# Two-layer decoder trunk in one kernel: 20 sums over partitions as products with rounded ones, and no product of zeros ahead of a chunk

## The chip, the cores and the metric

The kernel runs on one core of one Trainium2 chip. The metric is device time in microseconds (us) of one execution; the time of a kernel is the median of its runs. The engines are PE (TensorE, matrix products; PEld is its weight load), DVE (VectorE), ACT (ScalarE), POOL (GpSimd) and SP (SyncE, which here issues DMAs).

## What is computed

A trunk of two layers over 16 meta tokens and 512 tokens, with model width 1024 and hidden width 2816. Each layer is a gated FFN, a token mixer and another gated FFN; layer 0 mixes by chunked gated linear attention with four heads, layer 1 by sliding-window attention on one shared key/value set. Everything is float32. What matters here is that every sub-layer is wrapped in two norms over the model width, and that the four heads of the linear attention have a norm of their own:

```
def rmsnorm(x, g):
    y = x * rsqrt(mean(x * x, axis=-1) + EPS);  return y * g
def swiglu(x, w_in, w_out):
    gate, up = split(x @ w_in, 2);  return (silu(gate) * up) @ w_out
h = h + 0.5 * rmsnorm(swiglu(rmsnorm(h, g[0]), ...), g[1])      # first FFN
h = h + rmsnorm(mixer(rmsnorm(h, g[2])), g[3])
h = h + 0.5 * rmsnorm(swiglu(rmsnorm(h, g[4]), ...), g[5])      # second FFN
# inside the linear attention, per head:  o = rmsnorm(o, g_head) * silu(r)
```

## The kernel before

Features lie on the 128 partitions and tokens along the free axis, so the residual `H` is eight tiles of 128 features by 528 tokens. Tokens are worked in two groups: 272 and 256 in layer 0 (`L0`), 256 and 256 in layer 1 (`L1`). Precision of float32 in the matrix products comes from splitting: each operand `x` is kept as a part in the rounded format (`F32R`, printed fp32r) and a remainder, `x - rounded(x)`, also in that format. ACT makes the first with a Copy, DVE the second with a subtraction. A product is then three matmuls (`mm3s`): high by high, low by high, high by low.

The norm factors are not applied ahead of a product but behind it. `Operand.build` splits `H` times the gain; `Operand.sumsq` squares each of the eight tiles on ACT and adds them up on POOL (L394) into one tile `acc` of 128 partitions; `Operand.factors` waits `FACT` = 5 us of the planned clock and calls `roots`. That one sums `acc` over the partitions with a product by a matrix of `ones` in plain float32 (tile `st_...` on the PSUM side), and behind it takes the reciprocal root on ACT (L375, L376) and refines it on DVE (L377 to L379). The result `R` scales what comes out of the projections. There are six such operands with factors of their own (l0f0, l0m, l0f1, kv, l1m, l1f1) of two groups each: 12 sums. The four heads of the linear attention make 8 more (`st_go`, in `core`, behind `square_into`). The norms on the way back into the residual (`Residual.run`, `st_post`) use `roots` too.

The FFNs work their first four hidden tiles plainly (`x_first`, `x_units`) and the other 18 in three chunks with a scheme of seven products in place of eight (class `Strassen`). It keeps five PSUM banks per chunk: two each of `a` and `c`, which alternate between hidden tiles, and one `d`. For each hidden tile, `head` forms product 11 in `a` and copies it on ACT into `d` (L871); `body` adds product 12 onto `d` and takes Silu of it into `g1` (L880). Before the first tile of a chunk, the constructor multiplies zeros by zeros into `d`, once for each of the 12 chunks, so that what ACT writes there can be added onto by the products behind it.

The order of work is written out by hand: a planned clock (`flow`) advances with each matmul issued, and generators that `yield` a delay put ACT, DVE and POOL work between the matmuls at planned times. Each engine's own list is then ordered by what a planner holds to be ready, so that work issued later can stand ahead. Each engine is then given its list, with waits on semaphores in it.

Of the kernel before, what the change touches and what calls it, by code (L numbers as in the profile page):

```python
# [9 lines left out]
F32 = mybir.dt.float32  # L10
F32R = mybir.dt.float32r
I32 = mybir.dt.int32
AF = mybir.ActivationFunctionType
ALU = mybir.AluOpType
AX = mybir.AxisListType

P = 128
D = 1024
# [9 lines left out]
L0 = [(0, 272), (272, 256)]  # L28
# [11 lines left out]
FACT = 5.0  # L40
# [87 lines left out]
def trunk_kernel(ctx: ExitStack, tc, a, out):  # L128
    nc = tc.nc
    pe, act, dve, pool, sp = nc.tensor, nc.scalar, nc.vector, nc.gpsimd, nc.sync  # L130
    flow = Flow()

    cp = ctx.enter_context(tc.tile_pool(name="cp", bufs=1))
    rp = ctx.enter_context(tc.tile_pool(name="rp", bufs=RAWS))
    hp = ctx.enter_context(tc.tile_pool(name="hp", bufs=SLOTS))
    sm = ctx.enter_context(tc.tile_pool(name="sm", bufs=3))
# [5 lines left out]
    ident = cp.tile([P, P], F32, name="ident")  # L142
    ones = cp.tile([P, P], F32, name="ones")
    eps = cp.tile([P, 1], F32, name="eps")
    zeros = cp.tile([P, P], F32R, name="zeros")

    def ps(name):
        return pp.tile([P, 512], F32, tag="ps", name=name)

    def pair_tile(name, dt=F32R):  # L150
        return hp.tile([P, 2, TOK], dt, tag="pair", name=name)
# [5 lines left out]
    def flat(t):  # L157
        return t.rearrange("p a t -> p (a t)")
# [5 lines left out]
    def mm(o, lhs, rhs, start=True, stop=True, onto=False):  # L164
        inst = pe.matmul(o, lhs, rhs, start=start, stop=stop, skip_group_check=onto)  # L165
        n = 1
        for d in rhs.shape[1:]:
            n *= d
        flow.clock += n / 2400 if rhs.dtype == F32R else max(n / 600, 0.12)
        return inst  # L170
# [161 lines left out]
    def next_pair():  # L332
        used[0] += 1
        prefetch()
        flow.until(lambda: len(loaded) >= used[0])
        return loaded[used[0] - 1]
# [27 lines left out]
        mm3s([(o, w)], j, x, g, start, stop)  # L364


    def roots(sums, n, c, name, dst=None, dim=D):
        s = ps(f"st_{name}")
        for i, t in enumerate(sums):
            mm(s[:, :n], ones, t[:, :n], i == 0, i == len(sums) - 1)  # L370
        yield SUMMED
        if dst is None:
            dst = (sums[1] if sums[1:] else acc_tile(f"root_{name}"))[:, :n]
        q, y = sums[0][:, :n], dst
        act.activation(y, s[:, :n], AF.Abs_reciprocal_sqrt, scale=1.0 / dim, bias=eps)  # L375
        act.activation(q, y, AF.Square, scale=dim ** -0.5)  # L376
        dve.scalar_tensor_tensor(q, s[:, :n], dim * 1e-6, q, op0=ALU.add, op1=ALU.mult)  # L377
        dve.tensor_scalar(q, q, -0.5 * c, 1.5 * c, op0=ALU.mult, op1=ALU.add)
        dve.tensor_tensor(y, q, y, op=ALU.mult)  # L379
        return y, s  # L380


    def acc_tile(name):
        return sm.tile([P, 272], F32, tag="acc", name=f"acc_{name}", bufs=6)

    def square_into(sums, src, i, count, name, apart=False):
        n = src.shape[-1]
        if i == 0 or apart and i == count - 1:
            sums.append(acc_tile(name))
            act.activation(sums[-1][:, :n], src, AF.Square)  # L390
            return
        t = sm.tile([P, 272], F32, tag="sq", name=f"sq_{name}", bufs=2)
        act.activation(t[:, :n], src, AF.Square)  # L393
        pool.tensor_tensor(sums[0][:, :n], sums[0][:, :n], t[:, :n], op=ALU.add)  # L394
# [6 lines left out]
    class Operand:  # L401


        def __init__(self, name, gv, groups, rt=None):
            self.name, self.gv, self.groups, self.tiles = name, gv, groups, [None] * KD
            self.ready = set()
            self.rt = rt
            self.rjob = [None] * len(groups)
            self.built = [Job(None) for _ in groups]
            self.accs = [[] for _ in groups]  # L410
# [17 lines left out]
        def factors(self, gi):  # L428
            if self.rt is None:
                self.rt = sm.tile([P, TOK], F32, tag="R", name=f"R_{self.name}", bufs=2)  # L430
            o, n = self.groups[gi]
            yield FACT
            yield from roots(self.accs[gi], n, 1.0, f"{self.name}_{o}", self.rt[:, o : o + n])

        def need(self, gi, k):
            flow.until(lambda: (gi, k) in self.ready)
# [2 lines left out]
    class Residual:  # L439
# [4 lines left out]
        def run(self, gi, g, sums):  # L444
            o, n = g
            nxt = self.nxt
            yield 1.8
            r, s = yield from roots(sums, n, self.c, f"post_{self.name}{gi}")
            if nxt is None:
                yield from self.store(gi, g, r)  # L450
                return
            for k in range(KD):
                h, y = H[:, k, o : o + n], Y[:, k, o : o + n]
                c = k % 2 * 256
                t = s[:, c : c + n] if n <= 256 else ps(f"t_{self.name}{gi}{k}")[:, :n]
                dve.scalar_tensor_tensor(t, y, self.gain(k), r, op0=ALU.mult, op1=ALU.mult)
                dve.tensor_tensor(h, t, h, op=ALU.add)  # L457
                nxt.build(gi, k)
                nxt.sumsq(gi, k)
                yield 1.0  # L460
            nxt.rjob[gi] = flow.spawn(nxt.factors(gi))
            nxt.built[gi].finish(flow)
# [374 lines left out]
    class Strassen:  # L837
        def __init__(self, z, halves):
            self.z, (self.o, self.n) = z, halves[0]
            self.a, self.c = ([ps(f"{nm}{used[0]}_{i}")[:, : self.n] for i in range(2)] for nm in "ac")  # L840
            self.d = ps(f"d{used[0]}")[:, : self.n]
            q = self.n // 4
            zz = zeros[:, :q].unsqueeze(1).to_broadcast([P, 4, q])
            mm(self.d.rearrange("p (a c) -> p a c", c=q), zeros, zz)
            self.tiles = []

        def product(self, bank, t, left, right, first):
# [13 lines left out]
        def head(self, hid):  # L861
            t = Job(None)
            t.pair, t.hid, i = next_pair(), hid, len(self.tiles) % 2
            self.tiles.append(t)
            t.a, t.c, t.name = self.a[i], self.c[i], used[0]
            scratch = flat(pair_tile(f"c{t.name}", F32))
            n = self.n
            t.u2, t.g1, t.v = (scratch[:, i * n : (i + 1) * n] for i in range(3))
            t.h = scratch[:, n : 3 * n]
            self.product(t.a, t, "11", "11", True)  # L870
            act.activation(self.d, t.a, AF.Copy)  # L871
            return t

        def body(self, t):
            self.product(t.c, t, "s1", "t1", True)
            act.activation(t.v, t.c, AF.Copy)
            self.product(t.a, t, "s2", "t2", False)
            act.activation(t.u2, t.a, AF.Copy)  # L878
            self.product(self.d, t, "12", "21", False)
            act.activation(t.g1, self.d, AF.Silu)  # L880
            self.product(t.a, t, "s3", "t3", False)
            dve.tensor_tensor(t.v, t.a, t.v, op=ALU.add)

# [28 lines left out]
    def gla(x, finish):  # L912
        set_ahead(10)
        with tc.tile_pool(name="gp", bufs=1) as gp:
# [61 lines left out]
            def core(h, before):  # L976
# [10 lines left out]
                for i in range(2):  # L987
                    p = ps(f"pv{h}_{i}")
# [32 lines left out]
                p = ps(f"pk{h}")  # L1021
# [13 lines left out]
                p = ps(f"pa{h}")  # L1035
# [14 lines left out]
                s = flat(pair_tile(f"st{h}", F32))[:, :1024].rearrange("p (b v) -> p b v", v=256)  # L1050
                p = ps(f"ps{h}_0")
# [11 lines left out]
                for i in range(2):  # L1063
                    vs = slice(i * P, (i + 1) * P)
                    p = ps(f"po{h}_{i}")
                    for b in range(4):
                        o = p[:, b * P : (b + 1) * P]
# [7 lines left out]
                accs = []  # L1075
                for gi, (o, n) in enumerate(L0):
                    accs.append([])
                    for i in range(2):
                        square_into(accs[gi], Y[:, 2 * h + i, o : o + n], i, 2, f"go{h}_{gi}")
                yield 2.0  # L1080
                def scale(gi, o, n):
                    r, _ = yield from roots(accs[gi], n, 0.5, f"go{h}_{gi}", dim=256)
                    dve.tensor_tensor(
                        yy[:, :, o : o + n], yy[:, :, o : o + n],
                        r.unsqueeze(1).to_broadcast([P, 2, n]), op=ALU.mult,
                    )
# [50 lines left out]
            for h in range(HEADS):  # L1137
                cores.append(flow.spawn(core(h, [gate] + late + cores[h - 1 : h])))
                if h + 1 < HEADS:
                    kk = [("k", h + 1), ("q", h + 1), ("v", 2 * h + 2), ("v", 2 * h + 3)]  # L1140
                    late = x_units(x, 4, L0, lambda i, g, p, kk=kk: evac(*kk[i], g, p))
# [206 lines left out]


    dve.memset(ones, 1.0)  # L1350
    act.activation(zeros, ones, AF.Copy, scale=0.0)
    act.dma_start(vec, a["vec"])
    x = Operand("l0f0", lambda k: gain(0, 0, k), L0)

# [12 lines left out]
    def second():  # L1367
        for k in range(KD):
            x.build(1, k)
            yield 0.4  # L1370
        x.rjob[1] = flow.spawn(factors(1))
# [14 lines left out]
    for c in (0, 512):  # L1386
        for k in range(c // 128, c // 128 + 4):
            x.build(0, k)
            if k % 4 < 2:
                split_part(k % 4, raws[k % 4][c // 512], 512)  # L1390
    x.rjob[0] = flow.spawn(factors(0), 2.0)
    dma_end[0] = 1.0
    load_unit()
# [131 lines left out]
```

## Time and profile before

| | before |
|---|---|
| median of 3 runs | 1869.87 us (1869.71 to 1871.39) |
| the profiled execution | 1868.85 us |
| its span, first to last instruction | 1867.0 us |
| PE busy | 1848.1 us (99%) |
| DVE, ACT, POOL busy | 1349.2, 1002.0, 315.2 us (72%, 54%, 17%) |
| mean granted TensorE clock | 0.999 |

The span is what the profile sees; 1.85 us of the profiled execution lie around it. Busy times of engines overlap. L165 is the line of the helper that issues every matmul, so products are told apart by their tiles. A sum in plain float32 appears as two records of one matmul each.

### The profile page before, as it was taken

How to read it: one execution, taken by the hardware profiler on the slowest of the kernel's cores; microseconds unless marked ns; L12 is line 12 of the kernel's file. 1: busy time of each engine (PE TensorE's matmuls, PEld its weight loads, DVE VectorE, ACT ScalarE, POOL GpSimd, SP SyncE). 2: the span in 40 equal slices, each digit the busy share in tenths (PEclk: the TensorE clock that was granted, in tenths of full speed). 3: DMA queues.
4: the chain of work that ended last, by engine and by line, in shares of the span. 5: the costliest groups of instructions: out<-in, count | busy, mean ns of one | idle time of the engine just before them, and what ended most of it. 6: DMA issues, size and time to landing. Idle time of an engine off the chain costs nothing.

```text
span 1867.0 us, 36799 instructions
## 1 busy us (share of the span) xinstructions
PE 1848.1 (99%) x14158; PEld 1762.7 (94%) x14158; DVE 1349.2 (72%) x2679; ACT 1002.0 (54%) x2179; POOL 315.2 (17%) x370
## 2 busy tenths in 40 slices
PE   8999999999999999999999999999999999999998
PEld 8999999999999999999999898989977898989897
DVE  7884757786574988484789685758799589858484
ACT  6662636564465666262665563636556566626363
POOL 2101010320001310101033011010353231010101
PEclk9999999999999999999999999999999999999999
DMA  5655655312113255555652356565411215565561
GB/s 198 146 152 143 153 147 159 125 58 80 46 58 114 69 136 154 137 150 149 163 165 58 102 150 161 145 161 158 131 56 48 80 37 134 161 150 155 145 175 46
DMA packets 132528, 231.31 MB, mean 124 GB/s; under 512 B 14848, under 2 KB 26624, under 8 KB 132352
## 3 DMA queue, kind: packets, MB, share of 16 engines
q1 hardware_dynamic: 111328, 191.07, 32.2%
q0 software_dynamic: 20736, 37.76, 12.9%
q8 instruction: 111, 1.82, 0.4%
q14 instruction: 65, 0.53, 0.1%
q10 hardware_dynamic: 288, 0.13, 0.0%
HBM read 226.80 MB, written 2.10 MB: 123 GB/s over the span
## 4 chain that ended last, share of the span: by engine, by line
PE 89%; DVE 6%; ACT 3%; issue 1%; DMA 0%; POOL 0%; SPq 0%; DVEq 0%; ACTq 0%; POOLq 0%
PE y L165 29%; PE a L165 21%; PE x L165 17%; PE c L165 10%; PE d L165 5%; PE o L165 1%; PE e L165 1%; PE yt L165 1%; PE po L165 1%; DVE w L238 1%; ACT w L237 1%; PE sc L165 1%; DVE H L457 1%; PE ps L165 0%; PE pt L177 0%
## 5 line engine op out<-in xcount | busy, mean ns | idle before, releaser
L270 POOL DMA_DIRECT2D raw<-in_w_in x144 | 125.8, 940 | 973.8 <-DMA raw<-in_w_in 366.1
L165 PE MATMUL y<-hidl0f,w 128*128 128x256 f32 (+1 forms) x2112 | 260.4, 285 | 0.0
L165 PEld LDWEIGHTS y<-hidl0f,w 128*128 128x128 f32 x2112 | 258.6, 188 | 0.2
L238 DVE TENSOR_TENSOR w<-raw,w 128x512 fp32r<-128x512 f32 x376 | 241.3, 669 | 23.6 <-ACT w L237 21.4
L265 DVE TENSOR_TENSOR w_s<-raw,w_s 128x512 fp32r<-128x512 f32 x288 | 195.3, 689 | 80.5 <-ACT w_s L264 78.3
L264 ACT ACTIVATE w_s<-raw 128x512 fp32r<-128x512 f32 x288 | 177.6, 625 | 110.4 <-DVE raw L280 69.9
L165 PE MATMUL y<-hidl1f,w 128*128 128x512 f32 (+1 forms) x1200 | 233.1, 354 | 0.0
L165 PEld LDWEIGHTS y<-hidl1f,w 128*128 128x128 f32 x1200 | 195.1, 188 | 32.8 <-DVE w L238 0.3
L237 ACT ACTIVATE w<-raw 128x512 fp32r<-128x512 f32 x376 | 206.6, 586 | 33.6 <-PE y L165 27.9
L265 DVE TENSOR_TENSOR w<-raw,w 128x512 fp32r<-128x512 f32 x216 | 145.6, 688 | 37.1 <-ACT w L264 35.1
L264 ACT ACTIVATE w<-raw 128x512 fp32r<-128x512 f32 x216 | 130.5, 621 | 46.5 <-PE y L165 45.4
L165 PE MATMUL x<-x_l0m,w 128*128 128x272 f32 (+1 forms) x1152 | 151.9, 289 | 0.0
L165 PEld LDWEIGHTS x<-x_l0m,w 128*128 128x128 f32 x1152 | 143.4, 188 | 1.6 <-ACT R_l0m L375 0.4
L585 DVE TENSOR_TENSOR Y<-y,Y 128x256 f32<-128x256 f32 (+2 forms) x160 | 75.6, 479 | 83.8 <-PE y L165 83.6
L165 PE MATMUL a<-zl0f_t,w_s 128*128 128x264 f32 x864 | 117.2, 285 | 0.0
L165 PE MATMUL a<-zl1f_t,w_s 128*128 128x256 f32 x864 | 114.6, 282 | 0.6 <-ACT c L878 0.4
L165 PEld LDWEIGHTS a<-zl0f_t,w_s 128*128 128x128 f32 x864 | 110.1, 188 | 0.0
L165 PEld LDWEIGHTS a<-zl1f_t,w_s 128*128 128x128 f32 x864 | 107.2, 188 | 1.7 <-ACT c L878 1.6
L394 POOL TENSOR_TENSOR acc_post<-acc_post,sq_post 128x256 f32<-128x256 f32 (+1 forms) x72 | 61.2, 850 | 275.8 <-ACT sq_post L393 272.9
L165 PE MATMUL x<-x_l0f,w 128*128 128x256 f32 (+1 forms) x768 | 98.3, 290 | 6.8 <-ACT w L237 5.9
L165 PEld LDWEIGHTS x<-x_l0f,w 128*128 128x128 f32 x768 | 96.4, 192 | 7.7 <-ACT w L237 5.9
L165 PE MATMUL x<-x_l1f,w 128*128 128x256 f32 (+1 forms) x576 | 92.1, 320 | 0.0
(386 smaller groups left out, 3364.5 us busy)
## 6 DMA issues: line engine op xcount, KB each, us to landing
raw<-in_w_in SPq DMA_DIRECT2D x424, 256.0 KB, 3.7
raw<-in_w_in POOLq DMA_DIRECT2D x144, 256.0 KB, 4.8
raw<-in_w_out SPq DMA_DIRECT2D x96, 256.0 KB, 3.5
raw<-in_w_last SPq DMA_DIRECT2D x48, 256.0 KB, 3.4
raw<-in_gla_in SPq DMA_DIRECT2D x48, 256.0 KB, 3.1
raw<-in_w_out SPq DMA_DIRECT2D x64, 128.0 KB, 2.9
raw<-in_gla_out SPq DMA_DIRECT2D x16, 256.0 KB, 2.8
raw<-in_w_q SPq DMA_DIRECT2D x16, 256.0 KB, 3.9
```

The source lines that it names most:

```text
L165: inst = pe.matmul(o, lhs, rhs, start=start, stop=stop, skip_group_check=onto)
L237: act.activation(w[:, 0, :m], raw[:, :m], AF.Copy)
L238: hold(dve.tensor_tensor(w[:, 1, :m], raw[:, :m], w[:, 0, :m].bitcast(F32), op=ALU.subtract))
L264: act.activation(w[:, 0, :512], src, AF.Copy)
L265: dve.tensor_tensor(w[:, 1, :512], src, w[:, 0, :512].bitcast(F32), op=ALU.subtract)
L270: pool.dma_start(dst, src, accum_op=ALU.add)
L394: pool.tensor_tensor(sums[0][:, :n], sums[0][:, :n], t[:, :n], op=ALU.add)
L457: dve.tensor_tensor(h, t, h, op=ALU.add)
L585: dve.tensor_tensor(y, p[:, :n], y, op=ALU.add)
```

## The change

`zeros` gives way to `rounded`, a 128x128 tile of ones in the rounded format. A new `sum_parts` splits a sum of squares into the rounded part (ACT) and the remainder (DVE), and `roots` can take these two parts: two matmuls in the rounded format in place of one in plain float32. `Operand.factors` makes the parts 3.5 us of planned clock after its start and issues the products 1.5 us later, in all the 5 us of before. The head norms make both groups' parts 1.2 us after the squares and issue the products 1.4 us after that, where they had waited 2.0. `Residual.run` is left as it is. In `Strassen` the product of zeros is gone; for the first tile of a chunk ACT copies product 11 into `g1` instead of `d`, product 12 opens `d`, and DVE adds the two before the Silu.

```diff
-    zeros = cp.tile([P, P], F32R, name="zeros")
+    rounded = cp.tile([P, P], F32R, name="rounded")
...
-    def roots(sums, n, c, name, dst=None, dim=D):
+    def roots(sums, n, c, name, dst=None, dim=D, parts=None):
         s = ps(f"st_{name}")
-        for i, t in enumerate(sums):
-            mm(s[:, :n], ones, t[:, :n], i == 0, i == len(sums) - 1)
+        if parts is None:
+            for i, t in enumerate(sums):
+                mm(s[:, :n], ones, t[:, :n], i == 0, i == len(sums) - 1)
+        else:
+            for i in range(2):
+                mm(s[:, :n], rounded, parts[:, i, :n], i == 0, i == 1)
         yield SUMMED
...
+    def sum_parts(total, n, name):
+        t = sm.tile([P, 2, 272], F32R, tag="parts", name=f"parts_{name}", bufs=2)
+        act.activation(t[:, 0, :n], total[:, :n], AF.Copy)
+        dve.tensor_tensor(t[:, 1, :n], total[:, :n], t[:, 0, :n].bitcast(F32), op=ALU.subtract)
+        return t
...  # Operand.factors
-            yield FACT
-            yield from roots(self.accs[gi], n, 1.0, f"{self.name}_{o}", self.rt[:, o : o + n])
+            yield FACT - 1.5
+            parts = sum_parts(self.accs[gi][0], n, f"{self.name}_{o}")
+            yield 1.5
+            yield from roots(self.accs[gi], n, 1.0, f"{self.name}_{o}", self.rt[:, o : o + n], parts=parts)
...  # Strassen.__init__
-            q = self.n // 4
-            zz = zeros[:, :q].unsqueeze(1).to_broadcast([P, 4, q])
-            mm(self.d.rearrange("p (a c) -> p a c", c=q), zeros, zz)
...  # Strassen.head
-            act.activation(self.d, t.a, AF.Copy)
+            t.opens = len(self.tiles) == 1
+            act.activation(t.g1 if t.opens else self.d, t.a, AF.Copy)
...  # Strassen.body
-            self.product(self.d, t, "12", "21", False)
-            act.activation(t.g1, self.d, AF.Silu)
+            self.product(self.d, t, "12", "21", t.opens)
+            if t.opens:
+                dve.tensor_tensor(t.g1, self.d, t.g1, op=ALU.add)
+            act.activation(t.g1, t.g1 if t.opens else self.d, AF.Silu)
...  # gla core, head norms
-                yield 2.0
+                yield 1.2
+                parts = [sum_parts(accs[gi][0], n, f"go{h}_{gi}") for gi, (o, n) in enumerate(L0)]
+                yield 1.4
                 def scale(gi, o, n):
-                    r, _ = yield from roots(accs[gi], n, 0.5, f"go{h}_{gi}", dim=256)
+                    r, _ = yield from roots(accs[gi], n, 0.5, f"go{h}_{gi}", dim=256, parts=parts[gi])
...
-    act.activation(zeros, ones, AF.Copy, scale=0.0)
+    act.activation(rounded, ones, AF.Copy)
```

## The prediction, made before the change was run

> **What bounds the kernel now.** I read the page from the top: shares of busy time, slices, the chain that ended last.
>
> ```profile
> PE 1848.1 (99%) x14158; PEld 1762.7 (94%) x14158; DVE 1349.2 (72%) x2679; ACT 1002.0 (54%) x2179; POOL 315.2 (17%) x370
> PE   8999999999999999999999999999999999999998
> PEclk9999999999999999999999999999999999999999
> PE 89%; DVE 6%; ACT 3%; issue 1%; DMA 0%; POOL 0%; SPq 0%; DVEq 0%; ACTq 0%; POOLq 0%
> ```
>
> PE is busy in every slice at a full clock, and 89% of the chain is PE's. So time taken off PE counts almost in full wherever nothing else takes its place, and a busier DVE or ACT counts only where PE comes to wait for it. The 9% of the chain on DVE and ACT says that there are such places. The waits of PE and the windows say where:
>
> ```profile
> PE x L165 <- ACT w L237: 5.9, 1, 5.9
> PE x L165 <- DVE w L238: 2.6, 4, 1.5
> core 0: us, PE busy (x) PEld busy (x) DVE busy (x) ACT busy (x) POOL busy (x), PEclk, DMA share, GB/s
> 475.00:479.00 4.00, 4.00 (x32) 3.87 (x31) 0.35 (x1) 2.66 (x5) 0.76 (x2) 1.00 0.01 4
> 960.00:1010.00 50.00, 49.77 (x407) 49.23 (x406) 45.51 (x110) 32.04 (x75) 22.17 (x28) 1.00 0.11 33
> 1340.00:1390.00 50.00, 48.27 (x348) 44.28 (x346) 46.04 (x108) 23.20 (x56) 30.47 (x35) 1.00 0.12 38
> 1500.00:1545.00 45.00, 44.65 (x315) 41.68 (x314) 41.57 (x92) 28.44 (x63) 17.63 (x21) 1.00 0.16 50
> 90.00:170.00 80.00, 80.00 (x657) 80.00 (x656) 57.14 (x107) 40.70 (x86) 8.78 (x11) 1.00 0.64 165
> ```
>
> The longest wait is the start. Inside a chunk (90 to 170) DVE is busy 57.14 of 80 us, 71%. Where one sub-layer hands over to the next, and the operands' norms are summed, it is 91% (960 to 1010), 92% (1340 to 1390) and 92% (1500 to 1545). Around a head's norm (475 to 479) it is nearly idle. A DVE instruction added in a chunk or at a head is covered; added at a handover it may not be.
>
> **What is removed from PE.** How many sums and products of zeros there are, by tile (a sum in plain float32 is two records), and then what they take, from the chain in order of time (start, length, what):
>
> ```profile
> L165 PE MATMUL st_l0f<-acc_l0f,ones x8: 378/386/393, 24.0 to 639.5; 128*128 128x272 f32 x4, 128*128 128x256 f32 x4
> L165 PE MATMUL st_l0m<-acc_l0m,ones x4: 379/392/483, 377.6 to 398.6; 128*128 128x272 f32 x2, 128*128 128x256 f32 x2
> L165 PE MATMUL st_kv<-acc_kv,ones x4: 378/386/392, 981.3 to 1002.2; 128*128 128x272 f32 x2, 128*128 128x256 f32 x2
> L165 PE MATMUL st_l1m<-acc_l1m,ones x4: 378/378/380, 1355.8 to 1376.7; 128*128 128x256 f32 x4
> L165 PE MATMUL st_l1f<-acc_l1f,ones x4: 377/378/379, 1518.5 to 1532.2; 128*128 128x256 f32 x4
> L165 PE MATMUL st_go<-acc_go,ones x16: 377/384/394, 444.7 to 541.8; 128*128 128x272 f32 x8, 128*128 128x256 f32 x8
> L165 PE MATMUL d<-zeros x12: 280/285/295, 80.5 to 1764.2; 128*128 128x264 f32 x6, 128*128 128x256 f32 x6
> ```
>
> ```profile
> 377.75 0.46 PE st_l0m L165 x2
> 378.20 3.90 PE x L165 x31
> 444.86 0.89 PE st_go L165 x4
> 1163.06 0.12 PE d L165
> 1164.60 1.40 PE c L165 x12
> ```
>
> Eight sums of 272 columns (2 l0f, 1 l0m, 1 kv, 4 heads) and twelve of 256. The durations of single records overlap, so the price is the pitch in the chain. A sum of 272 takes 0.46 us; its neighbours in the rounded format take 3.90 / 31 = 0.126 us each, so two of them 0.252. Saved: 0.208 us, eight times, 1.66 us. The four records of `st_go` are one sum of 272 and one of 256, so the latter takes 0.89 - 0.46 = 0.43 us; a product of 256 in the rounded format takes 1.40 / 12 = 0.117, two 0.233. Saved: 0.197 us, twelve times, 2.36 us. The twelve products of zeros take 0.12 us each, 1.44 us. Together **5.46 us** off PE. Product 12 of a first tile has as many matmuls as before, and no DMA or SP issue is moved.
>
> **What is added elsewhere.** Each of the 20 sums gets an ACT copy and a DVE subtraction of the same shape. Nearest rows, a split of the same size, and the same two-input kind of DVE work beside POOL's adds:
>
> ```profile
> L398 ACT ACTIVATE og<-rg 128x272 fp32r<-128x272 f32 x8 | 3.4, 428 | 5.7 <-DVE rg L1106 5.7
> L399 DVE TENSOR_TENSOR og<-rg,og 128x272 fp32r<-128x272 f32 x8 | 3.5, 441 | 1.2 <-ACT og L398 0.9
> L418 DVE SCALAR_TENSOR_TENSOR x_l0m<-H,vec,x_l0m 128x256 fp32r<-128x256 f32 x8 | 5.8, 731 | 0.6 <-ACT x_l0m L417 0.6
> L882 DVE TENSOR_TENSOR c<-a,c 128x264 f32<-128x264 f32 x36 | 15.4, 429 | 2.0 <-PE a L165 0.8
> ```
>
> So 0.43 us on ACT and 0.44 on DVE, 0.87 us in a row between POOL's last add and the product that reads it directly today. The upper end for DVE is 0.73. I take 0.44, because POOL's last add is over when the subtraction starts. [...]
>
> **First tiles of a chunk:** 12 DVE additions of 0.43 us (L882's row) put the Silu later, and they hold `d` until they have read it.
>
> ```profile
> 85.01 1.62 PE L165 MATMUL d<-zl0f,w 128*128 128x264 f32 x12
> 86.67 0.39 ACT L880 ACTIVATE c<-d 128x264 f32<-128x264 f32 x1
> 89.68 0.38 ACT L871 ACTIVATE d<-a 128x264 f32<-128x264 f32 x1 [0.50 <-PE a L165]
> ```
>
> The next writer of `d` is the copy at 89.68, 3.0 us behind the Silu's start; a DVE in a chunk that is 71% busy reads within that. Nothing. Without that cover the copy and everything behind it on ACT would start 0.43 us later, 12 times, 5.2 us as the far end, none of it on PE until product 12 of the second tile.
>
> **Heads:** the products are issued 2.6 us behind the squares instead of 2.0. DVE is busy 0.35 of 4 us there, and PE has x products to run. Nothing; far end 0.6 us for each of four heads, 2.4, if the last head's chain were what the output projection waits for.
>
> **Operands:** here a wait takes shape, because the sum stands right behind POOL's last add in two places:
>
> ```profile
> 376.64 0.76 POOL L394 TENSOR_TENSOR acc_l0m<-acc_l0m,sq_l0m 128x272 f32<-128x272 f32 x1 [0.44 <-ACT sq_l0m L393]
> 377.58 0.62 PE L165 MATMUL st_l0m<-acc_l0m,ones 128*128 128x272 f32 x2
> 377.66 0.47 ACT L375 ACTIVATE acc_post<-st_post_l0m,eps 128x256 f32<-128x256 f32 x1 [0.79 <-PE st_post_l0m L165]
> 980.20 0.88 POOL L394 TENSOR_TENSOR acc_kv<-acc_kv,sq_kv 128x272 f32<-128x272 f32 x1
> 981.30 0.62 PE L165 MATMUL st_kv<-acc_kv,ones 128*128 128x272 f32 x2
> ```
>
> POOL ends at 377.40; 0.87 us and some 0.05 for the hand-overs on top give 378.32, against a product that starts at 377.58: 0.74 us. For kv 981.08 + 0.92 = 982.00 against 981.30: 0.70. PE runs its list in order, so all x products behind wait too, and on ACT the copy that waits for POOL holds back the root of the returning norm (377.66) by at most its own 0.43 us; its reader is the DVE chain of the second group, which PE needs only after a whole group of x products. The planner can put x products ahead of the sum and so take the wait to nothing; I take it whole: 1.44 us. The other ten operand sums I take at nothing, since there POOL ends earlier and a copy that is ready goes into any hole of ACT's list. Their bound is in the first rival.
>
> **Sum:** 5.46 - 1.44 = 4.0 us less. The profiled execution, 1868.85 us (span 1867.0 and 1.85 around it), would become 1864.8; the median of the runs shown stands 1.02 us above it, so 1869.87 - 4.0 = **1865.9**. With none of the waits 1864.4, with 1.6 more of them 1867.5: the forecast's own range. About 0.2%, 3.7 us, is what a measurement of this kernel can tell from no change, so the forecast lies just beyond it.
>
> **Rival 1, slower: PE waits for a subtraction that is queued on a full DVE.** The product now stands behind two engines that run late in the handovers. The clearest place is the last one:
>
> ```profile
> 1531.98 0.59 PE L165 MATMUL st_l1f<-acc_l1f,ones 128*128 128x256 f32 x2
> 1535.48 0.69 DVE L238 TENSOR_TENSOR w<-raw,w 128x512 fp32r<-128x512 f32 x1
> 1536.59 0.47 ACT L375 ACTIVATE R_l1f<-st_l1f,eps 128x256 f32<-128x256 f32 x1
> 1377.57 0.40 DVE L1154 TENSOR_TENSOR q<-x,csq 128x256 f32<-128x256 f32 x1
> ```
>
> The root of l1f's second group starts 4.6 us behind its sum. If the parts queue as the root does, DVE makes the remainder behind the weight split that ends at 1536.17, at 1536.6, and PE waits 4.6 us. At l1m's second group (the second record of its sum starts at 1376.7, the sum so at 1376.5) DVE is through with its queue at 1377.97, the remainder is there at 1378.4: 1.9 us. These two, the 1.44 above and half as much as l1f's second group (2.3) for the other handovers make 10.2 us, 4.8 more than is saved: 1874.7. It decides from 5.46 us of waits, 0.46 for each of the 12 operand sums. For it: DVE at 91 to 92%. Against it: lists are ordered by readiness, so that a copy or a subtraction whose input is there can stand ahead of older work that still waits, and PE's list can take x products first. Chance 0.22.
>
> **Rival 2, within 0.2%: what PE saves at the handovers is given back there.** DVE paces them, PE's 2.4 us saved on operands (4 x 0.208 + 8 x 0.197) become longer waits for weight splits, such as the 1.5 us one among the waits of PE, while 1.62 (heads) and 1.44 (zeros) stay, less the 1.44 of the two waits: 1.6 us, 1868.3. For it: the same 92%. Against it: PE waits little there today (48.27 busy of 50). Chance 0.18.
>
> **Rival 3, faster still:** the lists are planned anew behind each change, and a new order drops some of PE's old waits (2.6 us for DVE's weight splits): 1864.4 - 2.6 = 1861.8. Chance 0.08. That the change doesn't do what it says, a sum of two products as dear as the one, speaks against the pitch of every x product; it is in rival 2.
>
> **The numbers.** Forecast 0.52, of which 0.42 ends beyond 0.2% and 0.10 within it. Faster 0.42 + 0.08 = 0.50, same 0.10 + 0.18 = 0.28, slower 0.22. The range takes in the forecast, rival 2 and the nearer half of rival 1, and stops at 1862.5, short of rival 3's full gain, and at 1873.0, short of rival 1's price.
>
> **What would show it.** `st_l0m`, `st_go` and the others as two records at a pitch of 0.12 to 0.13 us instead of 0.23; no `d<-zeros`; PE's busy time lower by about 5 us. The waits of PE would name a subtraction into `parts` with some 1.4 us in two waits, at the first groups of l0m and kv. Rival 1 shows as waits for `parts` of 2 us and more, above all near 1376 and 1532; rival 2 as no such waits, but more for DVE's weight splits (L238). A wait of ACT's copy L871 for DVE would show the cover of the first tiles gone. The forecast is wrong if PE's waits for `parts` pass 3 us or if PE's busy time falls by less than 4.

## The result and the profile after

| | before | after |
|---|---|---|
| median (runs) | 1869.59 us (22) | 1873.14 us (22) |
| lowest to highest | 1869.03 to 1872.06 | 1871.02 to 1875.66 |
| ratio of the two, 95% interval | | 1.0018 [1.0012, 1.0023] |
| the profiled execution, its span | 1868.85, 1867.0 us | 1872.58, 1870.8 us |

The change makes the kernel 0.18% slower, 3.5 us by the medians, where 4.0 us less was forecast. That is still inside the 0.2% that the prediction counts as no change, on the slower side, and 0.1 us above its range. First the shares of busy time of the kernel after, then the waits of its PE (what waits, for what: us in total, times, the longest):

```profile
PE 1845.8 (99%) x14146; PEld 1760.0 (94%) x14146; DVE 1358.7 (73%) x2711; ACT 1009.7 (54%) x2199; POOL 317.2 (17%) x370
```

```profile
PE x L165 <- ACT w L237: 6.1, 1, 6.1
PE x L165 <- DVE w L238: 3.1, 5, 1.4
PE pk L177 <- DVE f L1022: 2.5, 2, 2.0
PE st_kv L165 <- DVE parts_kv L390: 2.1, 1, 2.1
PE st_l1f L165 <- DVE parts_l1f L390: 0.4, 1, 0.4
PE st_go L165 <- DVE parts_go L390: 0.2, 1, 0.2
```

PE's busy time fell by 2.3 us, not by 5.5, and three waits for `parts` make 2.7 us, with one of 2.1 at the second group of kv. Another wait has grown that has nothing to do with a sum: the transposes `pk` of a head's keys wait 2.0 us for the DVE tile `f`. The kernel before has, in the same view:

```profile
PE pk L177 <- DVE f L1010: 1.3, 2, 0.9
```

Where the time goes is told by a comparison of places: the start of the same PE product in two profiles, one taken from the other. Each column is a stage of the kernel before, from the end of the stage to its left; each number is how much longer (+) than before that stage is in the kernel of the row, in us. The columns add up to the difference of the two spans. A star marks a stage in which the clock granted to TensorE fell to half for 3.4 us (below); the end of the span, at half from 1864.36 us on in before and from 1867.26 on in after, is not marked. The two sums of l0m lie in the stage of the linear attention, those of l0f0 in the first.

| | to l0m, 371.5 | linear attention, to 566.1 | FFN, to 975.7 | kv handover, to 1069.6 | attention and FFN, to 1506.0 | l1f handover, to 1575.8 | to the end | sum |
|---|---|---|---|---|---|---|---|---|
| after | +0.06 | -0.48 | -0.39 | +3.45* | +0.12 | +1.25 | -0.24 | +3.77 |
| e1 zeros only | -0.23 | +0.07 | -0.30 | +0.11 | -0.46 | -0.12 | -0.23 | -1.16 |
| e2 heads only | +0.35 | -2.00 | +0.40 | -0.22 | +1.77* | -0.04 | +0.06 | +0.32 |
| e3 operands only | +0.55 | -1.67 | -0.21 | +2.05 | +0.68 | +1.36 | -0.29 | +2.47 |
| e4 kv plain | +0.54 | -0.49 | -0.41 | -0.01 | +0.07 | +1.25 | -0.36 | +0.59 |
| e5 zeros, heads | -0.41 | -2.04 | +0.01 | -0.17 | +1.55* | -0.21 | -0.55 | -1.82 |
| e6 parts earlier | -0.26 | +0.25 | -0.15 | +0.80 | +1.47 | +1.25 | -0.28 | +3.08 |
| e7 products later | -0.01 | -2.76 | -0.27 | +0.34 | +0.46 | +0.92 | -0.22 | -1.54 |
| e8 no remainder | +0.96 | -0.68 | -0.63 | +0.09 | -0.25 | -0.43 | -0.45 | -1.39 |
| e9 parts unused | +1.05 | 0.00 | -0.20 | +0.62 | -0.53 | +1.13 | +0.03 | +2.10 |
| e10 later but l1m | -0.14 | -3.31 | -0.27 | +0.38 | +0.01 | +0.93 | -0.29 | -2.69 |
| e11 POOL remainder | +0.69 | +1.04* | -0.36 | +0.23 | -0.23 | +0.90 | -0.48 | +1.79 |
| e12 two operands | +0.22 | -2.77 | -0.65 | -0.02 | +1.66* | -0.13 | -0.26 | -1.95 |

Each row is one execution, so a few tenths mean nothing, in the first column least of all: the first matmul starts between 5.73 and 6.23 us of the span. In the row of after, the loss stands at kv (3.45) and at l1f (1.25), and the linear attention, where the heads should have gained, gives 0.48. The kv handover in the timeline (start, length, engine, line, operation; in brackets the idle time before it and what ended it):

```profile
999.12 0.42 ACT L389 ACTIVATE parts_kv<-acc_kv 128x256 fp32r<-128x256 f32 x1 [1.20 <-POOL acc_kv L404]
1001.40 0.28 PE L165 MATMUL st_kv<-parts_kv,rounded 128*128 128x256 f32 x1
1001.69 0.77 DVE L1193 TENSOR_TENSOR v<-x,R_kv 128x272 f32<-128x272 f32 x2
1002.38 0.47 DVE L428 SCALAR_TENSOR_TENSOR x_l1f<-H,vec,x_l1f 128x256 fp32r<-128x256 f32 x1
1002.47 1.01 POOL L1170 TENSOR_TENSOR k<-k,sh_k 128x272 f32<-128x272 f32 x1
1002.78 0.98 DVE L390 TENSOR_TENSOR parts_kv<-acc_kv,parts_kv 128x256 fp32r<-128x256 f32 x1
1003.81 0.58 PE L165 MATMUL st_kv<-parts_kv,rounded 128*128 128x256 f32 x1 [2.12 <-DVE parts_kv L390]
```

ACT's copy is ready at 999.54. The subtraction that needs only this copy and `acc_kv` starts at 1002.78, 3.24 us later, behind other work in DVE's list, and takes 0.98 us beside a POOL addition, against 0.42 at l1f (below). Of after's 20 subtractions the three that overlap POOL's work for 0.69 to 0.91 us take 0.88 to 0.98 us, three that overlap it for 0.2 take 0.50 to 0.51, and the other 14, beside an idle POOL, 0.42 to 0.44. PE, whose list has the second product here, stands for 2.12 us. Then the windows (length, busy time of PE, PEld, DVE, ACT and POOL with instructions, clock granted to TensorE, DMA share, GB/s):

```profile
1001.00:1004.00 3.00, 0.88 (x7) 0.67 (x7) 3.00 (x6) 1.98 (x5) 2.39 (x3) 0.95 0.00 0
1004.00:1007.20 3.20, 3.20 (x16) 3.20 (x17) 3.20 (x10) 2.74 (x6) 0.00 (x0) 0.52 0.14 45
```

PE is busy again in the second window, but at a granted clock of 0.52, and gets through 16 matmuls.

The parts of the change that were priced do what was said. In the timeline of PE, the sums of the first groups of l0m and kv:

```profile
379.26 0.41 PE L165 MATMUL st_l0m<-parts_l0m,rounded 128*128 128x272 f32 x2
982.30 0.41 PE L165 MATMUL st_kv<-parts_kv,rounded 128*128 128x272 f32 x2
```

Two records end 0.41 us after the first begins, where one lasts 0.28 (above): a pitch of 0.13, that of other products in the rounded format (0.126 for x). Neither waits. They stand at 379.26 and 982.30 instead of 377.58 and 981.30: x products were put ahead of them.

### The profile page after: what moved, and what is told of

The parts are those of the page before. It is cut to its first block, busy times and chain, and to the rows that moved or that the text cites. A ratio compares the mean times of both kernels' runs of the same rounds, so it can differ in the third digit from the quotient of the medians.

```text
span 1870.8 us, 36860 instructions
## 1 busy us (share of the span) xinstructions
PE 1845.8 (99%) x14146; PEld 1760.0 (94%) x14146; DVE 1358.7 (73%) x2711; ACT 1009.7 (54%) x2199; POOL 317.2 (17%) x370
## 3 DMA queue, kind: packets, MB, share of 16 engines
q8 instruction: 111, 1.82, 0.4%
```

## The experiments

Three theories at first. **A**: the loss is in the operand sums, at kv's second group: the wait, and the half clock behind it. **B**: any edit plans the lists anew, and that is what costs. **C**: the addition in the first tile of a chunk costs. Each change of time below is the kernel's ratio to the kernel before, run beside it on the same chip, times 1869.6; differences between two changed kernels ("under after") are of their medians.

**e1, zeros only.** `Operand.factors` and the head norms as before; only the product of zeros is gone.

> Only the product of zeros is taken out; all norms sum in plain float32 as before. Theory A (the loss is made at the operand sums, most of it at kv's second group, where PE waits 2.1 us for the remainder and then runs 3.4 us at half clock): the 12 products of zeros go, 1.4 us less than before, no new wait of PE over 0.3 us. Theory B (any edit has the lists planned anew, and the new order costs what it happens to cost): anywhere between 2 us less and 3 us more, with waits at places that have nothing to do with the edit. Theory C (the first tile's extra addition on DVE costs PE more than the product of zeros): 1 us more or worse, with waits behind a, c or d in the chunks.

Measured 1867.69 us (1867.16 to 1870.15), ratio 0.9991 [0.9982, 1.0]: 1.7 us less. C is out, and the term of 1.44 fits, though the interval reaches from 0 to 3.4 us.

**e2, heads only.** Operand sums plain, and the product of zeros back:

```diff
-            parts = sum_parts(self.accs[gi][0], n, f"{self.name}_{o}")
...
+            zz = zeros.unsqueeze(1).to_broadcast([P, self.n // 8, 8])
+            mm(self.d.rearrange("p (a c) -> p a c", c=8), rounded, zz)
...
-            t.opens = len(self.tiles) == 1
+            t.opens = False
```

> Only the eight head sums are made of two parts; operand sums are plain, and the products of zeros are back (12 of them, of the same width). Theory A: 1.6 us less than before if the last head's transposes of the keys wait for DVE no longer than before, about 0.4 us less if the 2.0 us wait that the changed kernel shows there comes with the head sums. Theory B: no relation to the 1.6 us, a wait elsewhere.

Measured 1867.68 us (1866.6 to 1869.27), ratio 0.999 [0.9982, 0.9999]: 1.9 us less, which fits the term of 1.62. Its profiled execution is its slowest run: the table shows the 2.00 us gained in the linear attention and 1.77 lost at 1386, where the clock was halved. The same two windows there in e2 and then in e1, which has the same work there:

```profile
1383.00:1386.00 3.00, 1.53 (x9) 1.01 (x8) 3.00 (x7) 0.00 (x0) 2.84 (x5) 1.00 0.00 0
1386.00:1389.40 3.40, 3.40 (x8) 1.77 (x6) 2.42 (x8) 1.85 (x7) 3.32 (x3) 0.51 0.62 169
```

```profile
1383.00:1386.00 3.00, 1.55 (x10) 0.75 (x8) 3.00 (x9) 0.00 (x0) 2.84 (x5) 1.00 0.00 0
1386.00:1389.40 3.40, 3.40 (x13) 2.13 (x13) 3.40 (x9) 1.14 (x5) 3.32 (x3) 1.00 0.54 153
```

Both kernels' PE was busy for half of the first window; in one the clock fell behind it, in the other it did not.

**e3, operands only.** Heads plain, and the product of zeros back.

> Only the twelve operand sums are made of two parts; heads are plain and the products of zeros are back. Theory A: 4 to 5 us more than before, with PE's wait for parts_kv of about 2 us at the second group of kv and a stretch of 3.4 us at a granted clock of 0.5 behind it. Theory B: the wait may fall on another operand or on none, and the time between 2 us less and 4 us more.

Measured 1871.95 us (1871.16 to 1874.05), ratio 1.0014 [1.0005, 1.0022]: 2.6 us more, where 2.4 us of PE's time are saved. So the loss is in the operand sums, as A has it. Its wait at kv and the windows:

```profile
PE st_kv L166 <- DVE parts_kv L391: 2.1, 1, 2.1
```

```profile
1001.00:1004.00 3.00, 0.95 (x8) 0.89 (x8) 3.00 (x9) 1.74 (x4) 1.69 (x2) 1.00 0.01 3
1004.00:1007.20 3.20, 3.20 (x29) 3.20 (x28) 3.17 (x10) 3.17 (x8) 0.00 (x0) 1.00 0.30 90
```

The same wait, no half clock: 29 matmuls in the second window against 16. Its kv stage is 2.05 us longer than before, after's 3.45. By these two executions the 2 us are the wait's own and the other 1.4 the clock's, and the clock does not fall each time.

**e4, kv plain.** As after, with kv's two sums in plain float32:

```diff
+            if self.name == "kv":
+                yield FACT
+                yield from roots(self.accs[gi], n, 1.0, f"{self.name}_{o}", self.rt[:, o : o + n])
+                return
```

> The changed kernel, but kv's two operand sums are plain float32 as before. Theory A: the wait and the half clock are gone, some 3.5 us less than the changed kernel, so about 0.2 us less than before (1869.4); no stretch at half clock before the end. Theory B: another place takes over, the time stays within 1 us of the changed kernel's.

Measured 1868.91 us (1868.34 to 1871.73), ratio 0.9996 [0.9987, 1.0005]: 4.2 us under after. The kv stage is back at its old length (-0.01). But 1.25 us at l1f and the linear attention's missing gain are still there, so kv is not all.

**e5, zeros and heads.** As after, with all 12 operand sums plain.

> The changed kernel with all twelve operand sums put back to plain float32: no product of zeros, head sums of two parts. If the parts of the change add up when the operands are left out: 1.75 + 1.75 = 3.5 us less than before, 1866.0, faster than both kernels. If the head sums' gain is lost again beside the other edit (the 2.0 us wait of the last head's key transposes, which stood in the changed kernel and with kv plain but not with the head sums alone): about 2 us less than before.

Measured 1865.69 us (1864.84 to 1866.99), ratio 0.9979 [0.997, 0.9988]: 3.9 us less, about the sum of e1 and e2 (3.6). These two parts add up, and beat both kernels. After is 7.4 us above it by the medians. By the prediction the operand sums were to take 1.0 off: 4 x 0.208 + 8 x 0.197 = 2.4, less 1.44 of waits.

**e6, parts earlier.** Is the remainder too late because the copy and the subtraction are issued too late? The parts 3.5 us ahead of the products instead of 1.5:

```diff
-            yield FACT - 1.5
+            yield FACT - 3.5
...
-            yield 1.5
+            yield 3.5
```

> The changed kernel with an operand's parts asked for 2 us of planned clock earlier (3.5 us ahead of the products instead of 1.5); nothing else. Theory A1 (the remainder stands too late in DVE's list for its product; DVE as such has room): the wait for parts_kv falls under 0.5 us and the time to that of the kernel with kv plain or below, 1867.5 to 1869. Theory A2 (DVE is full at the handovers, so whatever is put in there makes PE wait for something): the wait for parts_kv goes, but waits for other DVE work of the same size come up, and the time stays at 1871 or above.

Measured 1872.73 us (1871.96 to 1874.99), ratio 1.002 [1.001, 1.0029]: no better than after. Its waits:

```profile
PE x L165 <- DVE w L238: 4.3, 5, 1.4
PE st_kv L165 <- DVE parts_kv L390: 0.5, 1, 0.5
PE pk L177 <- DVE f L1022: 2.5, 2, 2.0
```

The wait at kv is 0.5 us, and 1.2 us more wait for weight splits instead (4.3 against 3.1), one of them, of 1.3 us, at 1376.7. That is as A2 has it: what DVE does earlier for a sum it does later for a product.

**e7, products later.** The parts where they are, the products 4.0 us behind them (`yield 4.0`).

> The changed kernel with an operand's products issued 4.0 us of planned clock behind its parts instead of 1.5; the roots follow 2.5 us later. Theory A1: PE has other products to run in the meantime, the wait for parts_kv falls under 0.5 us, 1868 to 1870. Theory A2: as with the parts earlier, 1871 or above. A third possibility: the root comes too late for what waits for it, and PE waits for free banks or for the weights of the next products, up to 2.5 us for an operand.

Measured 1867.41 us (1866.91 to 1869.05), ratio 0.9989 [0.998, 0.9998]: 5.7 us under after, with the same products on PE and the same copies and subtractions. There is no wait for `parts_kv`, and `pk` waits 0.8 us instead of 2.0. One change in its computation is told in the expectation of e10.

**e8, no remainder; e9, parts unused.** Two ways in which the remainders could cost: **A1**, PE waits for a remainder that is late in DVE's list; **A2**, DVE is full at the handovers, and the work itself pushes the rest back. e8 leaves out the subtraction and the second product of the operand sums (`for i in range(1 + low)`, `low=False`). e9 makes the parts and sums plainly:

```diff
-            yield from roots(self.accs[gi], n, 1.0, f"{self.name}_{o}", self.rt[:, o : o + n], parts=parts)
+            yield from roots(self.accs[gi], n, 1.0, f"{self.name}_{o}", self.rt[:, o : o + n])
```

> The changed kernel, but an operand's sum is taken from its rounded part alone: the twelve subtractions on DVE and the twelve second products are left out, so the norms are less exact. Theory A1 and A2 alike: no PE wait for a remainder, so at least the 2.1 us of kv and the 0.4 of l1f go, and 12 x 0.12 = 1.4 us of products: below 1868. If the loss came from the ACT copy instead, the time would fall by the 1.4 us of products alone.

> The changed kernel, but an operand's parts are made by ACT and DVE and read by nobody: its sums are plain float32 products of the accumulated squares, as before. Zeros and heads as changed. It stands between the version with zeros and heads alone (1865.7) and the changed kernel (1873.1). Theory A1 (what costs is that PE's product stands behind the remainder): no wait for parts, 1865.5 to 1867. Theory A2 (what costs is the load, 12 copies and 12 subtractions in stages where DVE is 91 to 92% busy): no wait for parts either, but waits for weight splits and other DVE work as in the changed kernel, 1869 or more, since the 2.4 us of PE that the two rounded products save are gone too.

e8: 1867.38 us (1865.56 to 1868.83), ratio 0.9986 [0.9978, 0.9995]. e9: 1871.3 us (1870.2 to 1873.59), ratio 1.001 [1.0001, 1.0019]. The waits of e9, in which no product reads the parts:

```profile
PE x L165 <- DVE w L238: 3.2, 4, 1.4
PE pk L177 <- DVE f L1022: 2.5, 2, 2.0
PE x L165 <- DVE x_l1f L428: 0.3, 1, 0.3
```

e9 and e5 have the same products. Twelve copies and twelve subtractions that nobody reads make 5.6 us between them. So waiting for remainders (A1) is not all, and after would be slow without it. In e8, without the subtractions, l1f loses nothing (-0.43) where e9 loses 1.13 with them; 0.6 us of that difference is its shorter sums, two times 0.43 less 0.117.

**e10, later but for l1m.** As e7, with l1m's products 1.5 us behind their parts (`yield 1.5 if self.name == "l1m" else 4.0`).

> The changed kernel with the products of an operand 4.0 us of planned clock behind its parts, but for l1m, which keeps 1.5 (there a later root lets one projection be rotated ahead of its tables' scaling, as in the run with all products later). ACT and DVE work as in the changed kernel. Theory A1: no wait for parts_kv, near the 1867.4 of the run with all products later. Theory A2: that run was fast because its order around l1m was another one; with l1m as changed, waits for weight splits near 1377 and 1385 are back and the time is 1869 or more.

Measured 1866.99 us (1866.11 to 1868.13), ratio 0.9988 [0.9979, 0.9996], as e7. Its waits:

```profile
PE x L165 <- DVE w L238: 2.9, 4, 1.4
PE pk L177 <- DVE f L1022: 0.8, 1, 0.8
```

**e11, remainder on POOL.** The operand sums' subtraction on POOL instead of DVE (`eng.tensor_tensor(..., op=ALU.subtract)`, `eng=pool`).

> The changed kernel with an operand's remainder made by POOL in place of DVE; POOL has just made the last addition of the same sum, and its additions of this size take 0.73 to 1.0 us against 0.44 on DVE. Theory A1: the product still stands behind two engines, now with 0.3 to 0.5 us more in a row; waits at the first groups of l0m and kv of about 1 us each, none of 2 us at kv's second group: 1868 to 1870. Theory A2: DVE's load is as before the change, so no new waits for its work: 1864 to 1867, faster than both kernels, if the planner covers the longer chain with x products.

Measured 1870.28 us (1868.56 to 1871.43), ratio 1.0002 [0.9993, 1.0011]: 2.9 us under after. Kv has no loss. L1f still has 0.90, with 0.6 us of waiting for the remainder that POOL now makes, and `pk` waits as in after. Taking the subtraction off DVE gives back less than half of the 7.4 us.

**e12, two operands.** As e5, with l0m and l0f1 in parts as well, their products 4.0 us behind the parts.

> A version meant to beat both kernels: zeros and heads as changed; of the operands only l0m and l0f1, the two ahead of and behind the linear attention, are summed from parts, with the products 4.0 us of planned clock behind them; l0f0, kv, l1m and l1f1 are summed in plain float32. By the stage times of the run with the products later, these two operands save about 1.0 and 0.9 us against zeros and heads alone, while the others lose: 1863.8, 5.5 us less than before. If which order the planner makes of the last head decides (its key transposes waiting 0.85 or 2.0 us), the longer wait would bring it back to 1865 or more. No wait for parts over 0.3 us.

Measured 1865.18 us (1864.23 to 1866.85; 7 runs), ratio 0.9972 [0.996, 0.9983]. It is the fastest of all and 5.2 us under before, but its interval overlaps that of e5, and the 1863.8 expected was not reached. Whether these four sums bring anything is open.

## Why the prediction was wrong

**The step that failed** is the line "The other ten operand sums I take at nothing, since there POOL ends earlier and a copy that is ready goes into any hole of ACT's list". It prices ACT's copy and forgets DVE's subtraction behind it, and it takes the copy to be ready when its turn in the list comes. At kv's second group the copy was indeed early (999.54), and the subtraction queued for 3.24 us. At l0f0 and l1f the copy or the subtraction stood in its list ahead of other work, waited there for its own input and held that work up (shown below). The queue at kv is rival 1's mechanism, at a third place: it had named the second groups of l1f with 4.6 us (0.37 came) and of l1m with 1.9 (none came). Its price of 1874.7 was near for another reason than its own: PE's waits for `parts` came to 2.7 us, not 10.2. The bound given, "wrong if PE's waits for `parts` pass 3 us", was thus not even reached; the other one, PE's busy time falling by less than 4, was. That sign, too, is mixed: 16 matmuls at a granted clock of 0.52 keep PE busy for 3.20 us in after, where 29 do at 1.00 in e3.

Point by point:

- **What is removed** was right. 1.44 us for the zeros: 1.7 in e1. 1.62 for the heads: 1.9 in e2. Both, 3.06: 3.9 in e5. The cover of the first tiles held.
- **The 1.44 us of waits** at the first groups of l0m and kv did not come. The prediction had said that x products could be put ahead, and took the wait whole.
- **A wait was priced by its length.** Kv's 2.1 us cost 2.05 in e3 and 3.45 in after's profile, with 16 matmuls in the time of 29.
- **Work beside the path was given no price but a wait.** e9 shows 5.6 us for copies and subtractions that PE never waits for, with the order that goes with them. By the two rows of the table, e9 less e5, they stand in the opening (1.46), the linear attention (2.04), kv (0.79) and l1f (1.34); in the attention stage e5's profile has a half clock that e9's has not, so the rows differ by less in all (3.9) than the medians. The prediction's windows had shown 91 to 92% for DVE at the handovers, but rival 2 used that only for a gain given back, not for a loss. In the opening and at l1f the traces show how the loss is made, and it is for the most part not a lack of room.

In the opening ACT's list has the second group's copy ahead of the first group's root. ACT in e9, then in e5, where the first group's sum starts at 24.45 and at 24.20:

```profile
26.66 0.42 ACT L389 ACTIVATE parts_l0f<-acc_l0f 128x256 fp32r<-128x256 f32 x1 [1.22 <-POOL acc_l0f L404]
28.39 0.49 ACT L379 ACTIVATE R_l0f<-st_l0f,eps 128x272 f32<-128x272 f32 x1
```

```profile
25.47 0.49 ACT L379 ACTIVATE R_l0f<-st_l0f,eps 128x272 f32<-128x272 f32 x1
```

ACT stands idle until POOL has added up the second group, and the first group's root comes 3.94 us behind its sum instead of 1.27. For l0m the prediction had counted such a delay of a root as "at most its own 0.43 us" of the copy; here it is 2.7. e8, which has the copies without the subtractions, shows the same idle time (1.2 us) and 0.96 more in the opening. After has it too and is only 0.06 longer there, 0.4 us of shorter sums included, so its price differs from kernel to kernel.

At l1f the list of DVE is the same in e9 and e5, from the first group's norm to the second group's sum, but for the two subtractions. DVE in e9, then in e5:

```profile
1515.85 0.42 DVE L381 SCALAR_TENSOR_TENSOR acc_post<-st_post_l1f,acc_post 128x256 f32<-128x256 f32 x1
1517.02 0.42 DVE L390 TENSOR_TENSOR parts_l1f<-acc_l1f,parts_l1f 128x256 fp32r<-128x256 f32 x1 [0.74 <-ACT parts_l1f L389]
1517.36 0.28 DVE L382 TENSOR_SCALAR acc_post<-acc_post 128x256 f32<-128x256 f32 x1
```

```profile
1513.82 0.42 DVE L381 SCALAR_TENSOR_TENSOR acc_post<-st_post_l1f,acc_post 128x256 f32<-128x256 f32 x1
1514.28 0.37 DVE L382 TENSOR_SCALAR acc_post<-acc_post 128x256 f32<-128x256 f32 x1
```

The first subtraction stands ahead of the returning norm (`acc_post`) and waits 0.74 us for its copy, and DVE does nothing else meanwhile. All its work behind, the remainders `x_l1f` for PE among it, falls back 0.97 us against e5; the second subtraction adds 0.34. Together that is 1.31 of the 1.34 us by which the stage differs. All kernels with these subtractions on DVE (after, e3, e4, e6, e7, e9, e10) have this wait of 0.7 us and lose 0.9 to 1.4 us at l1f; e8, which has the copies alone, and those with plain sums there (e1, e2, e5, e12) lose nothing. e11, with the remainder on POOL, loses its 0.90 in another way, with a wait for that remainder.

- **A new order was counted as a gain only** (rival 3). In the linear attention it is a loss. The DVE timeline ahead of the last head's `f`, first after, then before:

```profile
521.91 0.75 DVE L1113 TENSOR_TENSOR rg<-x,R_l0m 128x272 f32<-128x272 f32 x2
522.83 0.78 DVE L1115 SCALAR_TENSOR_TENSOR rg<-rg 128x272 f32<-128x272 f32 x2 [0.17 <-ACT rg L1114]
523.52 0.89 DVE L1120 SCALAR_TENSOR_TENSOR rg<-rg,vec,Y 128x272 f32<-128x272 f32 x2
525.91 0.57 DVE L1022 TENSOR_TENSOR f<-f,qk 128x400 f32<-128x400 f32 x1
```

```profile
521.69 0.57 DVE L1010 TENSOR_TENSOR f<-f,qk 128x400 f32<-128x400 f32 x1
522.51 0.77 DVE L1099 TENSOR_TENSOR rg<-x,R_l0m 128x272 f32<-128x272 f32 x2
```

Before, `f` comes first and the gates' work (`rg`) behind it; after, the gates' work stands ahead of `f`, which starts 4.2 us later, though the change edits neither. This is theory B at one place. The table divides by it. The kernels with the heads in parts and `pk` waiting 0.8 or 0.9 us (e2, e5, e7, e10, e12) gain 2.0 to 3.3 us in the linear attention; those in which it waits 2.0 (after, e4, e6, e8, e9, and e11 but for its half clock) gain 0.7 at the most. e7, e10 and e12 have l0m's copies and subtractions as well and gain the most, so here the order takes the gain and not the added work. The wait alone is 1.1 to 1.2 us of that; the rest is not followed.

The books of after against e5 in medians then read: +5.6 for copies, subtractions and the order that goes with them (e9 less e5); -2.4 for PE's shorter sums, by the prediction's price; and what is left of the 7.4, about 4.2 us, for waiting on remainders and the clock behind it. That remainder is found by difference; e4, which takes kv's waiting away, is 4.2 under after. Part of it is the clock's: among the runs with a mean granted clock of 0.999 or more the medians are 1871.42 (after, 7 runs), 1870.70 (e9, 6 runs) and 1865.56 (e5, 10 runs), which leaves 3.1 us in place of 4.2, beside 2.7 us of PE's waits for `parts`.

PE's own wait for a remainder matters little at l1f (DVE and PE in after's timeline):

```profile
1535.99 0.42 DVE L390 TENSOR_TENSOR parts_l1f<-acc_l1f,parts_l1f 128x256 fp32r<-128x256 f32 x1
1536.47 0.39 PE L165 MATMUL st_l1f<-parts_l1f,rounded 128*128 128x256 f32 x1 [0.37 <-DVE parts_l1f L390]
```

PE waits 0.37 us here of the 1.25 that the stage loses, and e9 loses 1.13 without this wait. **Open** stays why `pk` waits 2.0 us in six of the 13 changed kernels and not in the others, and how much of e9's 0.79 us at kv is DVE's added time and how much a new order, since both changed there.

## What to carry to other kernels

Work moved to an engine that is off the path is priced in the stage where it lands, by what stands in front of it and behind it in that engine's list: here an instruction that came up before its input was there held up all that stood behind it (1.22 us on ACT in the opening and 0.74 on DVE at l1f, in e9), and that was not free even when nobody waited for its result (e9 is 5.6 us above e5). A product that gets a new producer needs room behind it in the order (e7 took 5.7 us off after by placing the products 2.5 us later, where e6, which moved the producer forward, took nothing). And a change of three parts that don't depend on each other is best taken apart: two of them gave 3.9 us here, of which the third took back nearly twice as much.

## What the hardware showed

**Behind a wait of 2 us TensorE's granted clock fell to half in some executions and not in others.** In after it fell to 0.50 behind the wait of 2.12 us, for 3.41 us in the granted clock's records, and cost 1.4 us over e3's wait of 2.05 us at the same place, behind which it stayed at 1.00. In e11 it fell behind `pk`'s wait and in after it did not, though the waits are alike. The timelines of e11 and then of after:

```profile
527.15 0.66 PE L177 MATMUL pk<-ident,f 128*128 128x128 f32 x4 [2.02 <-DVE f L1022]
```

```profile
526.53 0.66 PE L177 MATMUL pk<-ident,f 128*128 128x128 f32 x4 [2.02 <-DVE f L1022]
```

One difference between them stands in the traces. In the clock's records the stretches at full clock are whole multiples of 3.4133 us long: 1853.437 us in before (543 times), 993.278 and 860.159 in after (291 and 252), 515.413 in e11 (151), 1375.571 in e2 (403). In before and after every change of the clock stands on a grid of such steps that begins with the first record, at 10.92 us of the span in before and at 10.41 in after. The windows of that grid around kv's wait, in after and then in e3, which has two:

```profile
1000.28:1003.69 3.41, 1.40 (x12) 1.20 (x11) 3.41 (x8) 2.70 (x7) 3.03 (x4) 1.00 0.00 0
```

```profile
998.39:1001.80 3.41, 2.66 (x23) 2.45 (x21) 3.41 (x11) 3.39 (x9) 2.49 (x4) 1.00 0.00 0
1001.80:1005.21 3.41, 2.10 (x17) 2.10 (x18) 3.41 (x8) 2.12 (x5) 0.97 (x1) 1.00 0.01 2
```

And around `pk`'s wait, in e11 and then in after:

```profile
524.40:527.81 3.41, 1.40 (x13) 1.17 (x12) 3.41 (x10) 3.04 (x7) 0.00 (x0) 1.00 0.00 0
527.81:531.22 3.41, 3.41 (x19) 3.19 (x19) 2.74 (x7) 1.24 (x3) 0.00 (x0) 0.50 0.52 156
```

```profile
522.41:525.82 3.41, 2.11 (x18) 1.90 (x16) 3.24 (x10) 2.47 (x7) 0.00 (x0) 1.00 0.02 5
525.82:529.23 3.41, 2.70 (x26) 2.56 (x26) 3.41 (x9) 1.82 (x5) 0.00 (x0) 1.00 0.30 81
```

Where the clock fell, 2.01 us of idle time lie in one window and the fall is at its end; where it did not, the same wait is split over two windows, 0.75 and 1.31 us in e3, 1.30 and 0.71 in after. `pk`'s wait in e4 and e9 left 1.9 us of idle time in one window, and the clock did not fall. Idle time alone does not tell the cases apart: in e2, e5 and e12 the clock fell at 1383 to 1386, at the end of windows with 1.45 to 1.50 us of it, and in e7, with 1.77 us there, it did not. What decides is not shown.

The spread of one kernel's runs goes with this clock. After's runs have medians of 1871.42, 1872.74 and 1874.68 us at a mean granted clock of 0.999, 0.998 and 0.997 (7, 6 and 9 runs). Of the 33 runs of before beside e1 to e4, the 21 at 0.999 and over have 1869.10, the 9 at 0.998 have 1870.99 and the 3 at 0.997 have 1871.73. At 0.999 and over after is thus 2.3 us slower than before, not 3.5; the rest goes with a clock below that in 15 of its 22 runs against 12 of 33.
